# Seven products instead of eight for eight k tiles of an FFN down projection

## The chip, the cores and the metric

The kernel runs on one core of a Trainium2 chip. The metric is the device time of one execution in microseconds (us). TensorE (PE, with its weight loads PEld), VectorE (DVE), ScalarE (ACT), GpSimd (POOL) and SyncE (SP, here only a DMA queue) each work through their own instructions in program order and wait for one another at semaphores.

## The reference, cut to what matters

A decoder block of one layer, 512 tokens, model width 1024, FFN width 2816, all in fp32. The part around the change is the end of it:

```python
f_g, f_u = jnp.split(h2 @ w_ffn_in, 2, axis=-1)
x = x + gate2 * ((jax.nn.silu(f_g) * f_u) @ w_ffn_out)     # (512 x 2816) @ (2816 x 1024)
return rms_norm(x, final_norm_g)
```

`gate2` comes from `silu(c) @ w_ada + b_ada`, the last sixth of its columns.

## The kernel before, in words

The whole kernel is one stream of matmuls. To keep fp32 precision with the faster fp32r matmul, each operand is split into a high part (ACT copies the value to fp32r) and a low part (DVE subtracts the high part from the value), and each product is three matmuls: high by high, high by low, low by high (`mm3`, lines 51 to 55). So each operand block costs ACT one copy and DVE one subtraction before PE can use it. The order of the instructions on every engine is written out by hand; the framework adds the semaphores.

Weights come through a list `stream`. `issue` (line 72) starts the DMA of a chunk into one of three `raw` buffers, `prep` (line 95) makes its high part (line 110) and low part (line 114) in one of three `hi` and `lo` buffers, `ensure` (line 117) does both up to a given chunk, and `get` (line 142) prepares two chunks ahead of the one in use.

The first FFN projection is done, for its later columns, in a loop over q from -1 to 17 (line 1416). An iteration is one 256-column block of `w_ffn_in`, multiplied with the 512 tokens by the Winograd form of Strassen's algorithm: both operands are cut into 2 x 2 blocks, eight added or subtracted blocks are formed, and seven products (`sprod`, line 1410, 12 matmuls of 256 columns each) take the place of eight. The results gather in four PSUM banks, 0 to 3 in odd iterations and 4 to 7 in even ones; some are copied by ACT from one bank to the next (lines 1450 and 1461), others evacuated and added by DVE (lines 1468 to 1476). The operands of iteration q + 1 are made while PE works on q (`s_prep`, line 1275, four steps placed between the products). Even iterations give silu of the gate, odd ones the product `gq` of gate and up part: 22 tiles of 128 rows, 512 tokens wide. Tiles 12 to 15, 16 to 19 and 20, 21 lie together in the buffers E5, E6 and F1.

`last_mod` (line 1320) adds up the last section of `w_ada` in iterations 1 to 8, in buffer E6. `last_gate` (line 1329) splits it, and `sec_tasks` (line 364) sums it over the partitions with two matmuls in one bank (the number in `mbank`) and lets DVE add the bank to `gate_b[2]`; it is done twice, for two halves of 512 columns.

The second FFN projection is lines 1504 to 1554. For each half h of the 1024 output columns it goes through eleven chunks of `w_ffn_out`, two k tiles (256 rows) of 512 columns each. In a chunk each of the four token tiles `tk` gets 2 x 3 matmuls of 512 columns into its own bank (`opt_a_mm`, line 689): 24 matmuls. The first half uses banks 4 to 7. In it `g_split` (line 1355) makes high and low parts of the `gq` tiles just ahead of their use, in buffers that `GHOME` names, and `last_gate` and `sec_tasks` stand behind chunks 3, 5, 6 and 8. At its end `resid` (line 1100) multiplies each bank by the gate, adds it to the residual and lets ACT sum the squares. The second half uses banks 0 to 3, and its last token tile is done as two halves of 256 columns in banks 3 and 7. Its last three chunks are taken token tile by token tile, so that the residual, the final norm and the store of one tile (`finish`, line 1498) go on while PE works on the next.

The first weight chunks of the second projection are issued in iterations 16 and 17 (lines 1425 to 1427), and `s_prep(18)` prepares two of them and four `gq` tiles between the products of iteration 17.

Of the kernel before, what the change touches and what calls it, by code (L numbers as in the profile page):

```python
# [16 lines left out]
S = 512  # L17
D = 1024
# [10 lines left out]
def block_kernel(ctx: ExitStack, tc: tile.TileContext, x, positions, w_ada, b_ada, w_in,  # L29
# [267 lines left out]
    def t512(name, dt=F32):  # L297
        return base.tile([128, 512], dt, name=name, tag="t512", bufs=3)
# [898 lines left out]
    P.dma_start(gate_b[2], rows_bcast(b_ada[0, 5 * D:6 * D], D))  # L1197


    gq = {}  # L1200

    def gtile(m):
        if m not in gq:
            if m < 12:
                gq[m] = base.tile([128, S], F32, name="gq", tag=f"S1_{m + 8 if m < 8 else m - 8}", bufs=1)
            else:
                n = 4 if m < 20 else 2
                t = ffn[0].tile([128, n, S], F32, name="gq", tag=("E5", "E6", "F1")[(m - 12) // 4], bufs=1)
                for e in range(n):
                    gq[m + e] = t[:, e]  # L1210
        return gq[m]

    fs = {}
# [61 lines left out]
    def s_prep(q):  # L1275

        if q >= NQ:
            return [(lambda: ensure(wseq[w_out_at]), lambda: None), (lambda: None, lambda: g_split(1)),
                    (lambda: None, lambda: g_split(3)), (lambda: ensure(wseq[w_out_at + 1]), lambda: g_split(4))]
        ra, rb = sraw[q]  # L1280
        d = sw[q] = {}
        A11, A21, A12, A22 = ra[:, :, 0], ra[:, :, 1], rb[:, :, 0], rb[:, :, 1]

        def a0():
            d["A"] = tuple(base.tile([128, 4, 128], F32R, name="sa", tag=f"S1_{4 + 2 * (q % 2) + e}", bufs=1)
                           for e in range(2))
            A.activation(d["A"][0], A11, AF.Copy)

        def d0():
            V.tensor_add(A21, A21, A22)  # L1290
            V.tensor_sub(d["A"][1], A11, f(d["A"][0]))
            V.tensor_sub(A11, A21, A11)

        def a1():
            d["B"] = s_pair(q, 0)
            A.activation(d["B"][0], rb, AF.Copy)

        def d1():
            V.tensor_sub(d["B"][1], rb, f(d["B"][0]))
            V.tensor_sub(rb, rb, A11[:, :, None, :].to_broadcast([128, 4, 2, 128]))  # L1300

        def a2():
            d["C"] = s_pair(q, 1)
            A.activation(d["C"][0], ra, AF.Copy)

        def d2():
            V.tensor_sub(d["C"][1], ra, f(d["C"][0]))
# [30 lines left out]
    GHOME = [("S1_4", "S1_5"), ("S1_6", "S1_7"), "S2_0", "S2_1", "E2", None, "E4", None, "E1", None, "S2_4", "S2_5",  # L1338
             "E3", None, "S2_6", "S2_7", "S2_2", "S2_3", "E7", None, "E0", None]
    spare = []  # L1340

    def g_home(m):
        h = GHOME[m]
        if h is None:
            return spare.pop()
        if isinstance(h, tuple):
            return [base.tile([128, S], F32R, name="gs", tag=t, bufs=1) for t in h]
        if h[0] == "S":
            t = base.tile([128, 2, S], F32R, name="gs", tag=h, bufs=1)
        else:  # L1350
            t = ffn[0].tile([128, 4, S], F32R, name="gs", tag=h, bufs=1)
            spare.append((t[:, 2], t[:, 3]))
        return t[:, 0], t[:, 1]

    def g_split(upto):
        while len(gT) < min(upto, 22):
            m = len(gT)
            hi, lo = g_home(m)
            split(hi, lo, gq[m])
            gT[m] = (hi, lo)  # L1360


    pf = [[bank(b, "pf") for b in bs] for bs in ((0, 1), (2, 3))]
# [52 lines left out]
    for q in range(-1, NQ):  # L1416
        g, u = 2 + q // 2, q % 2
        d = sw[q]
        s_issue(q + 2)
        pre = s_prep(q + 1)  # L1420
        half_of = lambda t, e: tuple(v[:, :, e] for v in t)
        S2_, S1_, A12, A22, S4_, S3_ = (half_of(d[k], e) for k in "CBD" for e in range(2))
        R = [bank(k + 4 * (q % 2 == 0), "R")[:, :256] for k in range(4)]
        ps = [ffn[0].tile([128, 256], F32, name="ps", tag="rt", bufs=2) for _ in range(2)]
        if q >= NQ - 2:
            st["limit"] = W_FO[0][2] if q == NQ - 2 else 1 << 30
            ensure(st["prep"] - 1)
        t0, t1 = slice(0, 256), slice(256, 512)
        if u:
            dst = [gtile(2 * g + m) for m in range(2)]  # L1430
        else:
            fs[0], fs[1] = t512("fs"), t512("fs")
            dst = fs
        cur = dict(fs)

        def out_direct(m, p, u=u, dst=dict(enumerate([dst[0], dst[1]])), cur=cur):
            if u:
                V.tensor_mul(dst[m][:, t0], cur[m][:, t0], p)
# [11 lines left out]
        A.activation(R[1], R[0], AF.Copy)  # L1450
# [22 lines left out]
        V.tensor_add(dst[1][:, t1], R[3], ps[1])  # L1473
        sprod(R[1], S4_, HB[1, 1], False)
        out_late(1)
        V.tensor_add(dst[0][:, t1], R[1], ps[0])
# [5 lines left out]
    while left:  # L1482
        left.pop(0)()


    fng = ffn[0].tile([128, D], F32, name="fng", tag="F0", bufs=1)
    P.dma_start(fng, rows_bcast(final_norm_g, D))
    xo = []

    def scale_g(c0, n, tk):  # L1490
# [7 lines left out]
    def finish(tk):  # L1498
        A.activation(xo[tk][:, 640:], xo[tk][:, 640:], AF.Copy, scale=r2[:, tk:tk + 1])
        V.tensor_scalar(xo[tk][:, :640], xo[tk][:, :640], r2[:, tk:tk + 1], None, op0=OP.mult)  # L1500
        for c, q in ((slice(0, 640), SY), (slice(640, 1024), A)):
            q.dma_start(out[tk * 128:(tk + 1) * 128, c], xo[tk][:, c])

    for h in range(2):
        pb = [bank(4 - 4 * h + tk, "pfo") for tk in range(4)]
        pb.append(bank(7, "pfo") if h else None)
        ids = W_FO[h]
        for n_, i in enumerate(ids[:-3] if h else ids):
            kts = stream[i]["kts"]
            if h == 0:  # L1510
                g_split(kts[-1] + 1)
            hi, lo = get(i)
            if h == 0:
                g_split(kts[-1] + 4)
            for tk in range(4):
                if h and tk == 3:
                    for z in range(2):
                        c = slice(256 * z, 256 * z + 256)
                        opt_a_mm(pb[3 + z][:, :256], tk, hi[:, :, c], lo[:, :, c], kts, gT, 22)
                else:  # L1520
                    opt_a_mm(pb[tk], tk, hi, lo, kts, gT, 22)
# [11 lines left out]
        for tk in range(4):  # L1533
            for z in range(2) if tk == 3 else (None,):
                c = slice(0, 512) if z is None else slice(256 * z, 256 * z + 256)
                o = pb[tk] if z is None else pb[3 + z][:, :256]
                for i, (hi, lo) in zip(ids[-3:], ch):
                    opt_a_mm(o, tk, hi[:, :, c], lo[:, :, c], stream[i]["kts"], gT, 22)
# [65 lines left out]
```

## Time and profile before

| what | value |
|---|---|
| median of the 3 runs | 846.37 us (845.7 to 847.01) |
| the profiled execution's own time | 845.96 us |
| its span, first to last instruction | 844.2 us |
| mean granted TensorE clock | 0.998 |
| loop over q ends, second projection begins | 713.44 us from the span's start |
| first half of it ends, second begins | 775.41 us |
| last matmul starts | 836.86 us |

The profile was taken on one execution. Its rows in order of time read: start, duration (both us), engine, line of the kernel, operation, output<-inputs, shape, count, and in brackets the time that the engine was idle before and what ended that idle time. A row of a table by stage reads: stage, its length, the busy time of PE, PEld, DVE, ACT and POOL with the number of instructions, the granted TensorE clock, the share of DMA time and GB/s. The durations of matmuls overlap: the step from one start to the next says what a matmul costs, not its duration.

### The profile page before, as it was taken

To read this page: it belongs to the slowest core of one execution; us is meant where nothing else is said; L and a number is where in the kernel's file an instruction comes from. 1 tells how busy PE (TensorE), PEld (TensorE's weight loads), DVE (VectorE), ACT (ScalarE), POOL (GpSimd) and SP (SyncE) were. 2 spreads that over 40 slices of the span, in tenths; PEclk is the share of its full clock that TensorE was granted. 3 is DMA by queue.
4 is the path that set the end of the run, shared out by engine and by line. 5 is a ranking of instruction groups with operands and counts; after the bars stand their busy time and mean duration, and the time that the engine had idled before them with its cause. 6 is when DMAs were issued, how large, how long until landed. Compare 5 with 4: busy or idle time off the path is not lost.

```text
span 844.2 us, 12940 instructions
## 1 busy us (share of the span) xinstructions
PE 831.0 (98%) x5052; PEld 740.5 (88%) x5052; DVE 638.6 (76%) x1127; ACT 386.4 (46%) x680; POOL 118.6 (14%) x105
## 2 busy tenths in 40 slices
PE   7999999999999999999999999999999999999996
PEld 6888889988888888988888899999999999888885
DVE  7978799798899548886767579899998887446225
ACT  5664445322332236666333455655555555433222
POOL 2060022452354411002210000000000000000001
PEclk9999999999999999999999999999999999999999
DMA  9962362432346641146544033445433333332312
GB/s 299 307 188 78 89 200 78 125 99 81 117 142 187 197 150 51 26 127 233 178 138 149 1 125 100 150 154 163 159 102 115 111 117 107 101 100 75 103 47 99
DMA packets 95644, 109.09 MB, mean 129 GB/s; under 512 B 5584, under 2 KB 76240, under 8 KB 95584
## 3 DMA queue, kind: packets, MB, share of 16 engines
q1 hardware_dynamic: 92480, 101.37, 39.5%
q0 software_dynamic: 2384, 6.10, 2.0%
q8 instruction: 39, 0.64, 0.3%
q10 hardware_dynamic: 720, 0.82, 0.3%
q14 instruction: 21, 0.17, 0.1%
HBM read 105.90 MB, written 2.10 MB: 128 GB/s over the span
## 4 chain that ended last, share of the span: by engine, by line
PE 96%; DMA 1%; DVE 1%; issue 0%; SPq 0%; ACT 0%; POOLq 0%; POOL 0%; DVEq 0%
PE pb L53 9%; PE pb L55 9%; PE pb L54 9%; PE R L53 7%; PE R L54 7%; PE R L55 7%; PE pfo L55 5%; PE pfo L54 5%; PE pfo L53 5%; PE pav L54 2%; PE pav L53 2%; PE pav L55 2%; PE po L54 2%; PE pgb L53 2%; PE pgb L54 2%; PE pgb L55 2%
## 5 line engine op out<-in xcount | busy, mean ns | idle before, releaser
L110 ACT ACTIVATE hi<-raw 128x1024 fp32r<-128x1024 f32 (+2 forms) x93 | 96.1, 1037 | 135.7 <-PE pfo L55 67.7
L114 DVE TENSOR_TENSOR lo<-raw,hi 128x1024 fp32r<-128x1024 f32 (+2 forms) x53 | 65.4, 1239 | 75.0 <-ACT hi L110 74.9
L114 POOL TENSOR_TENSOR lo<-raw,hi 128x1024 fp32r<-128x1024 f32 x33 | 83.4, 2531 | 212.9 <-ACT hi L110 207.2
L53 PE MATMUL pb<-h,hi 128*128 128x512 f32 x192 | 76.4, 398 | 0.0
L54 PE MATMUL pb<-hl,hi 128*128 128x512 f32 x192 | 75.8, 395 | 0.0
L55 PE MATMUL pb<-h,lo 128*128 128x512 f32 x192 | 75.8, 395 | 0.0
L55 PE MATMUL pfo<-hi,gs 128*128 128x512 f32 (+1 forms) x198 | 73.0, 369 | 0.0
L53 PE MATMUL pfo<-hi,gs 128*128 128x512 f32 (+1 forms) x198 | 73.0, 369 | 0.0
L54 PE MATMUL pfo<-lo,gs 128*128 128x512 f32 (+1 forms) x198 | 73.0, 369 | 0.0
L53 PE MATMUL R<-tb,sx 128*128 128x256 f32 x160 | 45.2, 282 | 0.0
L54 PE MATMUL R<-tb,sx 128*128 128x256 f32 x160 | 45.1, 282 | 0.0
L55 PE MATMUL R<-tb,sx 128*128 128x256 f32 x160 | 45.0, 281 | 0.0
L55 PEld LDWEIGHTS pb<-h,lo 128*128 128x128 f32 x192 | 36.0, 188 | 8.7
L54 PEld LDWEIGHTS pb<-hl,hi 128*128 128x128 f32 x192 | 36.1, 188 | 8.3
L53 PEld LDWEIGHTS pb<-h,hi 128*128 128x128 f32 x192 | 36.0, 188 | 8.3
L55 PEld LDWEIGHTS pfo<-hi,gs 128*128 128x128 f32 x198 | 37.2, 188 | 6.8
L53 PEld LDWEIGHTS pfo<-hi,gs 128*128 128x128 f32 x198 | 37.3, 188 | 6.7
L54 PEld LDWEIGHTS pfo<-lo,gs 128*128 128x128 f32 x198 | 37.2, 188 | 6.7
L55 PE MATMUL R<-tb,lo 128*128 128x256 f32 x144 | 40.3, 280 | 0.0
L53 PE MATMUL R<-tb,hi 128*128 128x256 f32 x144 | 40.3, 280 | 0.0
L54 PE MATMUL R<-tb,hi 128*128 128x256 f32 x144 | 40.2, 279 | 0.0
L175 DVE SCALAR_TENSOR_TENSOR acc<-mraw,cols,acc 128x512 f32<-128x512 f32 x38 | 31.7, 835 | 9.3 <-DMA mraw<-in_w_ada_dram 8.5
(345 smaller groups left out, 2536.3 us busy)
## 6 DMA issues: line engine op xcount, KB each, us to landing
raw<-in_w_ffn_in_dram SPq DMA_DIRECT2D x44, 512.0 KB, 4.2
raw<-in_w_in_dram SPq DMA_DIRECT2D x40, 512.0 KB, 3.8
mraw<-in_w_ada_dram SPq DMA_DIRECT2D x22, 512.0 KB, 4.0
raw<-in_w_ffn_out_dram SPq DMA_DIRECT2D x22, 512.0 KB, 3.8
s<-in_w_ada_dram SPq DMA_DIRECT2D x30, 256.0 KB, 5.5
raw<-in_w_ada_dram SPq DMA_DIRECT2D x10, 512.0 KB, 4.5
raw<-in_w_proj_a_dram SPq DMA_DIRECT2D x8, 512.0 KB, 4.9
raw<-in_w_proj_b_dram SPq DMA_DIRECT2D x8, 512.0 KB, 3.5
```

The source lines that it names most:

```text
L53: T.matmul(o, wh, rh, start=start, stop=False, **kw)
L54: T.matmul(o, wh, rlo, start=False, stop=False, **kw)
L55: T.matmul(o, wlo, rh, start=False, stop=stop, **kw)
L110: A.activation(hi[:, :m], e["raw"][:, :m], AF.Copy)
L114: e["lo"].tensor_sub(lo[:, :m], e["raw"][:, :m], f(hi[:, :m]))
L175: V.scalar_tensor_tensor(o, w, cs[:, j:j + 1], o, op0=OP.mult, op1=OP.add)
```

## The change

Eight of the 22 k tiles (12 to 19) leave the stream of chunks. They are treated as a product of a 512 x 1024 matrix (tokens by those rows) and a 1024 x 1024 one, each cut into 2 x 2 blocks: A11, A12, A21, A22 of 256 tokens by 4 tiles, and B11 to B22 of 4 tiles by 512 columns. With S1 = A21 + A22, S2 = S1 - A11, S3 = A22 - S2 (in A11's place), S4 = A12 - S2 (in A21's place), T1 = B12 - B11, T2 = B22 - T1, T3 = B22 - B12, T4 = B21 - T2 (all by DVE, in place), seven products (`zprod`, 24 matmuls of 512 columns each) go into all eight banks: A11 B11, S1 T1, S2 T2, A12 B21, S3 T3, S4 B22, A22 T4. Three ACT copies and evacuations and two DVE additions join them (`z_copy`, `z_out`, `z_add`). Each of the four weight blocks is loaded as two pieces of two k tiles in buffers of its own. What was `s_prep(18)` is now `z_first`, which prepares B11, A11, S1 and T1 during iteration 17. The other 14 k tiles (seven chunks a half) are accumulated on top, with no first matmul that clears a bank. `last_gate` and `sec_tasks` move behind iterations 9 and 10, with both halves in bank 3. The first half uses banks 4, 7, 1, 2, the second 5, 6, 0, 3; since bank 7 holds no sum for the second half, ACT copies the upper 256 columns of bank 3 into it first. The first chunk of `w_ffn_out` is issued after the sixth product.

```diff
-    W_FO = [[add_w(w_ffn_out, [k, k + 1], 512 * h, 512) for k in range(0, 22, 2)] for h in range(2)]
+    KZ, KC = (list(range(12, 16)), list(range(16, 20))), list(range(12)) + [20, 21]
+    W_FO = [[add_w(w_ffn_out, KC[k:k + 2], 512 * h, 512) for k in range(0, len(KC), 2)] for h in range(2)]
...
         if q >= NQ:
-            return [(lambda: ensure(wseq[w_out_at]), lambda: None), (lambda: None, lambda: g_split(1)),
-                    (lambda: None, lambda: g_split(3)), (lambda: ensure(wseq[w_out_at + 1]), lambda: g_split(4))]
+            return z_first()
...
-    def last_gate(half):
-        ah, al = t512("ah", F32R), t512("al", F32R)
-        split(ah, al, acc[5, half])
-        acc[5, half] = al
-        sec_done.append((5, half, 0, ah))
+    def last_gate():
+        t = ffn[0].tile([128, 4, S], F32R, name="ahl", tag="E6", bufs=1)
+        for half in range(2):
+            ah, al = t[:, 2 * half], t[:, 2 * half + 1]
+            split(ah, al, acc[5, half])
+            acc[5, half] = al
+            sec_done.append((5, half, 0, ah))
...
+    ZW = {"T1": ("E2", "E4"), "T2": ("E1", "E3"), "T3": ("E0", "E7"), "T4": ("E2", "E4")}
+    ZA = {"A11": 0, "S1": 4, "S2": 6, "A12": 0, "S3": 4, "S4": 6, "A22": 0}
...
+    def w_hi(key, c, src):
...
+        for t, hi in z_parts(zr[src, c], zw[key, c][0]):
+            A.activation(hi, t, AF.Copy)
+
+    def w_lo(key, c, src):
+        for t, hi, lo in z_parts(zr[src, c], *zw[key, c]):
+            V.tensor_sub(lo, t, f(hi))
...
+    def a_hi(key):
+        za[key] = tuple(base.tile([128, 4, 256], F32R, name="za", tag=f"S2_{ZA[key] + e}", bufs=1) for e in range(2))
+        A.activation(za[key][0], a_block(AT_[key]), AF.Copy)
+
+    def a_lo(key):
+        V.tensor_sub(za[key][1], a_block(AT_[key]), f(za[key][0]))
...
+    def z_first():
+        return [(lambda: w_hi("B11", 0, "B11"), lambda: w_lo("B11", 0, "B11")),
+                (lambda: (a_hi("A11"), w_hi("B11", 1, "B11")), lambda: (a_lo("A11"), w_lo("B11", 1, "B11"))),
+                (lambda: None, lambda: (a_sum("S1"), w_sub("B11", "B12", "B11", 0))),
+                (lambda: (w_hi("T1", 0, "B11"), a_hi("S1")),
+                 lambda: (w_lo("T1", 0, "B11"), a_lo("S1"), w_sub("B11", "B12", "B11", 1)))]
...
         if q >= NQ - 2:
-            st["limit"] = W_FO[0][2] if q == NQ - 2 else 1 << 30
-            ensure(st["prep"] - 1)
+            z_issue(("B11", "B12")[q - NQ + 2])
...
+        if q == NQ - 1:
+            z_issue("B21")
...
+        if q == 9:
+            last_gate()
+        if q == 10:
+            mbank[0] = 3
+            sec_tasks(True)
+    z_issue("B22")
...
+    Z, ZB = {}, ((4, 7), (5, 6), (1, 2), (0, 3))
+
+    def zprod(k, ka, kw, start):
+        if start:
+            Z[k] = [bank(ZB[k][e], "pfo") for e in range(2)]
+        (ah, al) = za[ka]
+        for c in range(2):
+            wh, wl = zw[kw, c]
+            for e in range(2):
+                o = slice(e * 128, (e + 1) * 128)
+                for j in range(2):
+                    mm3(Z[k][e], (ah[:, 2 * c + j, o], al[:, 2 * c + j, o]), (wh[:, j], wl[:, j]),
+                        start and c + j == 0, c + j == 2, skip_group_check=True)
...
+    zprod(0, "A11", "B11", True)
+    w_hi("T1", 1, "B11")
+    w_lo("T1", 1, "B11")
+    while left:
+        left.pop(0)()
+    a_sum("S2")
+    z_copy(1, 0)
+    w_sub("B11", "B22", "B11", 0)
+    zprod(3, "S1", "T1", True)
+    a_hi("S2")
+    a_lo("S2")
+    w_hi("T2", 0, "B11")
+    w_lo("T2", 0, "B11")
+    w_sub("B11", "B22", "B11", 1)
+    w_hi("T2", 1, "B11")
+    w_lo("T2", 1, "B11")
+    z_out(3)
+    zprod(1, "S2", "T2", False)
+    a_hi("A12")
+    a_lo("A12")
+    for c in range(2):
+        w_hi("B21", c, "B21")
+        w_lo("B21", c, "B21")
+    for c in range(2):
+        w_sub("B12", "B22", "B12", c)
+    a_sum("S4")
+    w_hi("T3", 0, "B12")
+    z_copy(2, 1)
+    zprod(0, "A12", "B21", False)
+    w_lo("T3", 0, "B12")
+    a_sum("S3")
+    a_hi("S3")
+    a_lo("S3")
+    w_hi("T3", 1, "B12")
+    w_lo("T3", 1, "B12")
+    z_add(1, 3)
+    zprod(2, "S3", "T3", False)
+    a_hi("S4")
+    a_lo("S4")
+    for c in range(2):
+        w_hi("B22", c, "B22")
+        w_lo("B22", c, "B22")
+    for c in range(2):
+        w_sub("B11", "B21", "B11", c)
+    z_out(2)
+    zprod(1, "S4", "B22", False)
+    a_hi("A22")
+    a_lo("A22")
+    w_hi("T4", 0, "B11")
+    w_lo("T4", 0, "B11")
+    w_hi("T4", 1, "B11")
+    w_lo("T4", 1, "B11")
...
+    st["limit"] = 1 << 30
+    ensure(W_FO[0][0])
+    zprod(2, "A22", "T4", False)
+    g_split(2)
+    z_add(3, 2)
...
-        pb = [bank(4 - 4 * h + tk, "pfo") for tk in range(4)]
-        pb.append(bank(7, "pfo") if h else None)
+        pb = [Z[h][0], Z[h][1], Z[2 + h][0], Z[2 + h][1]]
         ids = W_FO[h]
+        if h:
+            pb.append(bank(7, "pfo"))
+            A.activation(pb[4][:, :256], pb[3][:, 256:], AF.Copy)
...
-            if h == 0 and n_ in (3, 6):
-                last_gate(n_ // 6)
-            if h == 0 and n_ in (5, 8):
-                mbank[0] = n_ // 8
-                sec_tasks(True)
```

More of the change, by code (lines that the diff above doesn't have):

```diff
@@ L1210, in gtile @@
                     gq[m + e] = t[:, e]
+                gz.append(t)
         return gq[m]
@@ L1355, in g_split, with z_issue @@
     def g_split(upto):
-        while len(gT) < min(upto, 22):
-            m = len(gT)
-            hi, lo = g_home(m)
+        while len(gT) < min(upto, len(KC)):
+            m = KC[len(gT)]
+            hi, lo = g_home(len(gT))
             split(hi, lo, gq[m])
             gT[m] = (hi, lo)
+    zr, zw, za = {}, {}, {}
+    ZW = {"T1": ("E2", "E4"), "T2": ("E1", "E3"), "T3": ("E0", "E7"), "T4": ("E2", "E4")}
+    ZA = {"A11": 0, "S1": 4, "S2": 6, "A12": 0, "S3": 4, "S4": 6, "A22": 0}
+    def z_issue(name):
+        kh, h = {"B11": (0, 0), "B12": (0, 1), "B21": (1, 0), "B22": (1, 1)}[name]
+        for c in range(2):
+            if name == "B11" or name == "B12" and c == 0:
+                t = base.tile([128, 2, S], F32, name="raw", tag="raw", bufs=RAWB)
+                ts = [t]
+            elif name == "B12":
+                ts = [ffn[0].tile([128, 2, S], F32, name="zraw", tag="F0", bufs=1)]
+            elif name == "B22":
+                ts = [base.tile([128, 2, S], F32, name="zraw", tag=f"S2_{2 + c}", bufs=1)]
+            else:
+                ts = [base.tile([128, 1, S], F32, name="zraw", tag=f"S1_{4 + 2 * c + e}", bufs=1) for e in range(2)]
+            k = KZ[kh][2 * c]
+            for t in ts:
+                n = t.shape[1]
+                SY.dma_start(t, w_ffn_out[k * 128:(k + n) * 128, h * 512:h * 512 + 512].rearrange("(j p) n -> p j n", p=128))
+                k += n
+            zr[name, c] = ts
@@ new lines, in z_parts @@
+    def z_parts(ts, *others):
+        o = 0
+        for t in ts:
+            n = t.shape[1]
+            yield (t,) + tuple(x_[:, o:o + n] for x_ in others)
+            o += n
+    def w_hi(key, c, src):
+        if key in ZW:
+            t = ffn[0].tile([128, 2, 2, S], F32R, name="zw", tag=ZW[key][c], bufs=1)
+            zw[key, c] = (t[:, 0], t[:, 1])
+        else:
+            zw[key, c] = tuple(base.tile([128, 2, S], F32R, name=n, tag=n, bufs=3) for n in ("hi", "lo"))
+        for t, hi in z_parts(zr[src, c], zw[key, c][0]):
+            A.activation(hi, t, AF.Copy)
@@ new lines, in w_lo, with w_sub, a_block @@
+    def w_lo(key, c, src):
+        for t, hi, lo in z_parts(zr[src, c], *zw[key, c]):
+            V.tensor_sub(lo, t, f(hi))
+    def w_sub(o, a, b, c):
+        (o_,), (b_,) = zr[o, c], zr[b, c]
+        for a_, ob, bb in z_parts(zr[a, c], o_, b_):
+            V.tensor_sub(ob, a_, bb)
+    def a_block(name):
+        kh, th = {"A11": (0, 0), "A21": (0, 1), "A12": (1, 0), "A22": (1, 1)}[name]
+        return gz[kh][:, :, th * 256:(th + 1) * 256]
+    AT_ = {"A11": "A11", "A12": "A12", "A22": "A22", "S1": "A21", "S4": "A21", "S2": "A11", "S3": "A11"}
@@ new lines, in a_hi, with a_sum @@
+    def a_hi(key):
[3 more added lines that the diff above has]
+        V.tensor_sub(za[key][1], a_block(AT_[key]), f(za[key][0]))
+    def a_sum(key):
+        a = {n: a_block(AT_[n]) for n in AT_}
+        if key == "S1":
+            V.tensor_add(a["S1"], a_block("A21"), a["A22"])
+        elif key == "S2":
+            V.tensor_sub(a["S2"], a["S1"], a["A11"])
+        elif key == "S4":
+            V.tensor_sub(a["S4"], a["A12"], a["S2"])
+        else:
+            V.tensor_sub(a["S3"], a["A22"], a["S2"])
@@ L1481, in block_kernel @@
             last_mod(q - 1)
[L1482 to L1487, printed above, removed]
+        if q == 9:
[4 more added lines that the diff above has]
+    z_issue("B22")
     xo = []
@@ new lines, in z_copy, with z_out, z_add @@
+    def z_copy(dst, src):
+        Z[dst] = [bank(ZB[dst][e], "pfo") for e in range(2)]
+        for e in range(2):
+            A.activation(Z[dst][e], Z[src][e], AF.Copy)
+    def z_out(src):
+        Z["s", src] = [t512("ps") for _ in range(2)]
+        for e in range(2):
+            A.activation(Z["s", src][e], Z[src][e], AF.Copy)
+    def z_add(dst, src):
+        for e in range(2):
+            V.tensor_add(Z[dst][e], Z[dst][e], Z["s", src][e])
+    zprod(0, "A11", "B11", True)
+    w_hi("T1", 1, "B11")
@@ new lines, in block_kernel @@
+    for c in range(2):
[17 more added lines that the diff above has]
+        w_lo("B22", c, "B22")
+    for c in range(2):
+        w_sub("B11", "B21", "B11", c)
@@ L1504, in block_kernel @@
+    z_out(2)
[6 more added lines that the diff above has]
+    w_lo("T4", 1, "B11")
+    fng = ffn[0].tile([128, D], F32, name="fng", tag="F0", bufs=1)
+    P.dma_start(fng, rows_bcast(final_norm_g, D))
+    st["limit"] = 1 << 30
[3 more added lines that the diff above has]
+    z_add(3, 2)
     for h in range(2):
-        pb = [bank(4 - 4 * h + tk, "pfo") for tk in range(4)]
@@ L1537, in block_kernel @@
                 for i, (hi, lo) in zip(ids[-3:], ch):
-                    opt_a_mm(o, tk, hi[:, :, c], lo[:, :, c], stream[i]["kts"], gT, 22)
+                    opt_a_mm(o, tk, hi[:, :, c], lo[:, :, c], stream[i]["kts"], gT, 22, False)
                 n = c.stop - c.start
```

19 lines of the change are left out of this document (9 added, 10 removed).

## The prediction

> **What bounds the kernel now.** I read the page first: TensorE is busy for 98% of the span and makes 96% of the chain that ended last.
>
> ```profile
> span 844.2 us, 12940 instructions
> PE 831.0 (98%) x5052; PEld 740.5 (88%) x5052; DVE 638.6 (76%) x1127; ACT 386.4 (46%) x680; POOL 118.6 (14%) x105
> PE 96%; DMA 1%; DVE 1%; issue 0%; SPq 0%; ACT 0%; POOLq 0%; POOL 0%; DVEq 0%
> ```
>
> Then the table by stage, cut at the marks of the code: one iteration of the loop over q (633.74 to 643.70 is q = 10, 693.50 to 703.46 is q = 16), the last one (q = 17), and the first chunk of the second FFN projection.
>
> ```profile
> 633.74:643.70 9.96, 9.96 (x86) 9.96 (x85) 8.90 (x14) 4.75 (x8) 0.00 (x0) 1.00 0.34 106
> 693.50:703.46 9.96, 9.96 (x86) 9.96 (x85) 8.90 (x14) 4.75 (x8) 0.00 (x0) 1.00 0.36 102
> 703.46:713.44 9.98, 9.98 (x87) 9.98 (x85) 5.11 (x8) 7.25 (x14) 0.55 (x1) 1.00 0.47 150
> 713.30:775.80 62.50, 62.50 (x273) 50.81 (x272) 32.85 (x47) 22.07 (x34) 0.00 (x0) 1.00 0.33 101
> ```
>
> The columns are PE, PEld, DVE, ACT, POOL busy. PE never waits; DVE has little room in the loop (8.90 of 9.96) and much in the projection (32.85 of 62.50). So only PE work can be saved, and each us that PE is made to wait costs a us.
>
> **The saving.** Two rows twelve matmuls apart give the pitch of a 128x512 matmul:
>
> ```profile
> 829.67 0.40 PE L55 MATMUL pfo<-hi,gs 128*128 128x512 f32 x1
> ...
> 832.47 0.40 PE L55 MATMUL pfo<-hi,gs 128*128 128x512 f32 x1
> ```
>
> 2.80 / 12 = 0.2333 us. Eight k tiles cost 8 x 8 output tiles x 3 = 192 matmuls; seven products cost 7 x (4 k tiles x 2 token tiles x 3) = 168. The change removes 24: **-5.6 us**. Each product takes 24 x 0.2333 = 5.6 us of PE. Everything else is whether DVE, ACT and the DMAs deliver the operands on time.
>
> **What is added for DVE and ACT.** Their prices:
>
> ```profile
> 688.02 1.23 DVE L1299 TENSOR_TENSOR lo<-raw,hi 128x1024 fp32r<-128x1024 f32 x1 [1.45 <-ACT hi L1296]
> 689.28 1.23 DVE L1300 TENSOR_TENSOR raw<-raw 128x1024 f32<-128x1024 f32 x1
> 690.42 1.22 DVE L1307 TENSOR_TENSOR lo<-raw,hi 128x1024 fp32r<-128x1024 f32 x1
> 693.37 0.41 DVE L1438 TENSOR_TENSOR gq<-fs,R 128x256 f32<-128x256 f32 x1
> 693.70 0.42 DVE L1473 TENSOR_TENSOR gq<-R,ps 128x256 f32<-128x256 f32 x1
> 695.28 0.68 DVE L1290 TENSOR_TENSOR raw<-raw 128x512 f32<-128x512 f32 x1
> 695.88 0.69 DVE L1291 TENSOR_TENSOR sa<-raw,sa 128x512 fp32r<-128x512 f32 x1
> 704.42 1.04 ACT L110 ACTIVATE hi<-raw 128x1024 fp32r<-128x1024 f32 x1
> 705.37 0.37 ACT L1450 ACTIVATE R<-R 128x256 f32<-128x256 f32 x1
> 705.49 1.23 DVE L114 TENSOR_TENSOR lo<-raw,hi 128x1024 fp32r<-128x1024 f32 x1 [1.43 <-ACT hi L110]
> ```
>
> DVE on 1024 elements: 1.22 us, the next starts 1.14 after it; on 512: 0.60; on 256: 0.34. ACT on 1024: 1.05, next after 0.96. A consumer starts 0.03 after its producer (705.46 to 705.49). The operand blocks (4 x 256 tokens, or 2 x 512 weights) are all 1024 elements.
>
> I lay the queues out in program order from q = 17 (703.46), with ACT free at 704.42 and the first copy where L110 stands now. Without waits PE would end q = 17 at 713.44 and begin products two to seven at 719.04, 724.64, 730.24, 735.84, 741.44, 747.04.
>
> DVE's queue: low part of B11 (first half) 705.50 to 706.64; it waits for A11's high copy, which ACT does after the evacuation of product two (706.78 to 707.83); four large operations from 707.86 to 712.42; a wait for T1's high copy, which itself needs the fourth, to 713.61; three large to 717.03; five small ones of the loop to 718.95; T1's second low part, a small one, S2 and B22-T1 to 722.71; lows of S2 and T2 and a subtraction to 726.18; a wait for ACT; **T2's second low part at 727.37 to 728.59**. Then A12's low part at 729.39 (a wait again), four halves of B21 (2.4 us) to 732.93, three large (two B22-B12, S4) to 736.35, T3's low part and S3 (done 738.71), the wait for S3's high copy (738.74 to 739.79), and **S3's low part at 739.82 to 741.04**. In all 22 large x 1.14 = 25.1, four halves 2.4, six small 2.3 and waits for ACT of 5.7 us, from 705.50: 741.0.
>
> PE against it. A11·B11 and S1·T1 do not wait (T1's second low part, 720.2, is wanted at 722.1). S2·T2 waits for T2: 0.28 + 0.67 = 0.95. A12·B21 waits for B21's low part: 0.43. S3·T3 could begin at 737.21; its first matmul waits for S3's high copy until 739.82, its third for the low part until 741.07: 2.61 + 0.78 = 3.39. S4·B22 and A22·T4 then find their operands (745.7 and 751.5, wanted at 746.2 and 751.8). **+4.8 us**. Bounds: if all waits for ACT vanished (5.7) nothing of it is left, 0; if each large operation were followed after 1.26 us instead of 1.14, as 688.02 to 689.28 is, 22 x 0.12 = 2.6 more, 7.4. I take 4.8, since 1.14 is the commoner step.
>
> **The weight stream begins anew.** Now the first chunks of w_ffn_out lie ready early (SP issues them from 691.66 on); in the change the first chunk's raw buffer is T4's, free at 751.48 once its low part is made.
>
> ```profile
> 691.66 75.00 SPq L92 DMA_DIRECT2D raw<-in_w_ffn_out_dram  x15
> raw<-in_w_ffn_out_dram SPq DMA_DIRECT2D x22, 512.0 KB, 3.8
> s<-in_w_ada_dram SPq DMA_DIRECT2D x30, 256.0 KB, 5.5
> ```
>
> 751.48 + 3.8 to 4.2 lands at 755.4; copy 1.05, low part 1.22 (757.8), low part of the first g tile (758.4). PE ends its last product at 757.40, and does two matmuls meanwhile: **+0.6**, between 0 (a wait that the late products before it take up) and 2 (a landing after 5.5 us, the slower row). The second chunk needs its g tiles at 763.6 and 764.3; they end at 763.1 and 763.7, queued behind both lows: nothing, if all goes so.
>
> **The gate at q = 10.** last_gate and its four matmuls leave the projection, where each pair (0.47 us, no wait behind it) had its own bank and stage, and go behind q = 9 and q = 10. Both pairs use bank 3: the second waits for DVE's add of the first.
>
> ```profile
> 643.58 0.28 PE L55 MATMUL R<-tb,lo 128*128 128x256 f32 x1
> 643.70 0.28 PE L53 MATMUL R<-h,sa 128*128 128x256 f32 x1
> 643.89 0.41 DVE L1476 TENSOR_TENSOR fs<-R,ps 128x256 f32<-128x256 f32 x1
> 644.22 0.68 DVE L1290 TENSOR_TENSOR raw<-raw 128x512 f32<-128x512 f32 x1
> 747.46 0.69 DVE L377 TENSOR_TENSOR gate2b<-gate2b,mod 128x512 f32<-128x512 f32 x1 [2.39 <-PE mod L375]
> ```
>
> Pair one runs 643.70 to 644.17. The two splits (1.3 us of DVE) leave DVE some 0.3 late at that place, the rest is taken by its idle time; so the add runs 644.5 to 645.2: **+1.05**, between 0.8 (DVE not late) and 2 (late by all of the 1.3). The add also holds DVE's next step until pair two is added, 0.3 more than PE's own delay, within DVE's spare 1.06 us an iteration.
>
> **The second half (h = 1).** Its fourth token tile is split over banks 3 and 7, and bank 7's part must first be copied by ACT out of bank 3. In ACT's queue that copy stands behind the four squares of the first half's residual.
>
> ```profile
> 775.41 0.39 PE L53 MATMUL pfo<-hi,gs 128*128 128x512 f32 x1
> ...
> 779.53 0.28 PE L53 MATMUL pfo<-hi,gs 128*128 128x256 f32 x1
> 780.24 0.28 PE L53 MATMUL pfo<-hi,gs 128*128 128x256 f32 x1
> 780.19 0.63 ACT L1105 ACTIVATE rt<-xr 128x512 f32<-128x512 f32 x1 [1.67 <-DVE xr L1104]
> 780.82 1.99 ACT L110 ACTIVATE hi<-raw 128x1024 fp32r<-128x1024 f32 x2
> ```
>
> h = 1 begins at 775.41; PE wants bank 3 4.12 us later (779.53) and bank 7 at 780.24. The copy can run at 780.82, where L110 stands now, to 781.2. If matmuls into bank 3 wait for a reader of that bank's other half, PE waits 1.7 us; if not, 1.0. **+1.7**: the kernel gives the two halves banks of their own, so the trace shows no case of a shared one. The Trainium skill, PSUM — Partial Sum Buffer, section on bank collisions, says to guard by bank and not by address; by that rule it is 1.7, without it 1.0; no row here shows it.
>
> **Sum.** -5.6 + 4.8 + 0.6 + 1.05 + 1.7 = **+2.6 us**. The profiled execution took 845.96 us, of which 1.8 lie around the span; 845.96 + 2.6 = **848.6**. The median of the runs shown, 846.37, is 0.4 above that execution.
>
> **Rivals.**
> 1. *DVE keeps up, and the kernel is faster.* Place: DVE's queue from q = 17 to S3. Price: its waits for ACT, 5.7 us in my layout, would not arise, the products would not wait, and the sum is -5.6 + 0.6 + 1.05 + 1.7 = -2.3: 843.7. It decides from 2.6 us less of such waits. For it: ACT is busy 4.75 of 9.96 us and could copy early. Against it: five of these copies need the subtraction just before them in DVE's own queue, or follow an evacuation.
> 2. *The waits at the banks do not come* (gate and copy cost nothing): -5.6 + 4.8 + 0.6 = -0.2: 845.8, no change. Against: both orders are written in the queues.
> 3. *The clock falls in the long wait* before S3·T3 (2.6 us, then 0.8). The trace has a fall after the last matmul:
>
> ```profile
> 836.86 0.28 PE L55 MATMUL pfo<-hi,gs 128*128 128x256 f32 x1
> 838.00:840.00 2.00, 0.00 (x0) 0.00 (x0) 1.32 (x5) 0.95 (x3) 0.66 (x1) 1.00 0.39 143
> 840.00:842.00 2.00, 0.00 (x0) 0.00 (x0) 0.11 (x1) 0.17 (x1) 0.00 (x0) 0.76 0.51 199
> 842.00:844.00 2.00, 0.00 (x0) 0.00 (x0) 0.00 (x0) 0.00 (x0) 0.00 (x0) 0.50 0.17 63
> ```
>
> Full until 840, mean 0.76 in the next 2 us, then 0.50: half speed from about 841.0, 3.9 us after PE's end (837.1). Two waits of 3.4 us in all are just short of that. If it falls for as long as it took to fall here, 3.9 us at half speed add 2.0: 850.6. The Trainium skill, TensorE: Matmul & The Clock Gate, Part 1, has the gate close after an idle window of about 3.4 us that runs freely; the trace's 3.9 agrees. By that rule 2.6 us is too short unless the wait grows by a third.
>
> **How the numbers follow.** Forecast +2.6 with its own bounds (846.5 to 851): 0.62. Rival 1 0.13, rival 2 0.15, rival 3 0.10. A measurement of this kernel tells about 0.2% (1.7 us) from no change. Faster is rival 1, 0.13; within 0.2% is rival 2 and 0.10 of the forecast's low end, 0.25; slower 0.62. The range begins between rivals 1 and 2, at 844.5, and ends at 852.0, above rival 3 and above the forecast with DVE's upper bound (848.6 + 2.6 = 851.2).
>
> **What would show it.** In the changed profile: PE rows of the seven products 0.233 apart, 168 of them; a PE wait of about 1 us for DVE before q = 11; one of 2 to 3 us before S3·T3 with DVE busy almost without pause and waiting only for ACT; the last w_ffn_out issues beginning after T4's low part; PE waiting for ACT in the first chunk of h = 1. The prediction is wrong if DVE is idle for long before S3, or if PE's wait there is under 1 us or the clock there is below 1.0.

## The result, and the profile after

The change made the kernel slower: 849.46 us (median of 6 runs, 849.1 to 850.88) against 846.71 us (6 runs of the kernel before, 845.7 to 847.1), a ratio of 1.0036 with a 95% interval of 1.0023 to 1.0049. The span of the profiled execution grew from 844.2 to 847.4 us, by 3.2; forecast were 2.6.

The page of the changed kernel answers the first lines of the page before:

```profile
span 847.4 us, 12890 instructions
PE 829.5 (98%) x5004; PEld 735.9 (87%) x5004; DVE 664.4 (78%) x1152; ACT 399.5 (47%) x696; POOL 118.4 (14%) x105
PE 89%; DVE 5%; DMA 2%; issue 1%; ACT 1%; SPq 1%; POOLq 0%; POOL 0%; DVEq 0%; ACTq 0%
```

PE has 48 matmul instructions fewer (24 full matmuls, and 24 more because 24 of the old ones stood as pairs of halves), but its share of the last chain fell from 96% to 89%: DVE, DMA and ACT are on it now. Where PE waits is read from its rows in order of time. A step from one start to the next above the pitch (0.233 us for 128x512, 0.119 for 128x256) is time lost; the bracket names who ended it. First the gate behind q = 10 (mod is its bank):

```profile
643.89 0.39 PE L377 MATMUL mod<-ahl,onesr 128*128 128x512 f32 x1
645.10 0.50 PE L376 MATMUL mod<-ahl,onesr 128*128 128x512 f32 x1 [0.82 <-DVE gate2b L379]
645.43 0.40 PE L377 MATMUL mod<-ahl,onesr 128*128 128x512 f32 x1
```

645.10 - 643.89 - 0.23 = 0.98 us for DVE's add of the first half, and 0.10 for the first matmul after the wait (0.33 instead of 0.23 to the next). Then the products S2 T2 and S3 T3 (zw is a weight operand, za a token operand):

```profile
729.92 0.39 PE L53 MATMUL pfo<-zw,za 128*128 128x512 f32 x1
730.74 0.50 PE L54 MATMUL pfo<-zw,za 128*128 128x512 f32 x1 [0.43 <-DVE zw L1408]
...
738.78 0.40 PE L55 MATMUL pfo<-hi,za 128*128 128x512 f32 x1
741.88 0.51 PE L53 MATMUL pfo<-zw,za 128*128 128x512 f32 x1 [2.71 <-ACT za L1425]
742.23 0.40 PE L54 MATMUL pfo<-zw,za 128*128 128x512 f32 x1
743.14 0.80 PE L55 MATMUL pfo<-zw,za 128*128 128x512 f32 x1 [0.52 <-DVE za L1428]
743.74 0.63 PE L53 MATMUL pfo<-zw,za 128*128 128x512 f32 x1
744.16 0.63 PE L54 MATMUL pfo<-zw,za 128*128 128x512 f32 x1
...
746.65 0.40 PE L54 MATMUL pfo<-zw,za 128*128 128x512 f32 x1
746.89 0.39 PE L55 MATMUL pfo<-zw,za 128*128 128x512 f32 x1
```

S2 T2 loses 1.1 us in two places (the second is shown). S3 T3 waits for S3's high copy and then for its low part: 2.87 + 0.12 + 0.68 = 3.7. And from 743.14 on the matmuls take 0.43 from start to start instead of 0.23, until 746.65: 1.6 us more. DVE's rows of that time show what it did meanwhile:

```profile
727.11 1.22 DVE L1414 TENSOR_TENSOR raw<-zraw,raw 128x1024 f32<-128x1024 f32 x1
729.46 1.23 DVE L1408 TENSOR_TENSOR zw<-raw,zw 128x1024 fp32r<-128x1024 f32 x1 [1.13 <-ACT zw L1404]
731.37 1.23 DVE L1428 TENSOR_TENSOR za<-gq,za 128x1024 fp32r<-128x1024 f32 x1 [0.69 <-ACT za L1425]
...
739.47 1.22 DVE L1439 TENSOR_TENSOR gq<-gq 128x1024 f32<-128x1024 f32 x1
741.87 1.23 DVE L1428 TENSOR_TENSOR za<-gq,za 128x1024 fp32r<-128x1024 f32 x1 [1.18 <-ACT za L1425]
```

It has no idle time but the turns to ACT, 1.13, 0.69 and 1.18 us in these rows (line 1439 forms S3, line 1428 its low part). ACT has more room: from 725 to 738 us it is busy for 7.82 us and DVE for 11.18, although ACT's copies and evacuations of banks are four steps of two banks each, not three. The last wait is that for the copy in the first chunk of the second half; these rows are of ACT and PE:

```profile
804.29 0.63 ACT L1107 ACTIVATE rt<-xr 128x512 f32<-128x512 f32 x1 [1.39 <-DVE xr L1106]
804.92 0.36 ACT L1686 ACTIVATE pfo<-pfo 128x256 f32<-128x256 f32 x1
803.61 0.40 PE L55 MATMUL pfo<-hi,gs 128*128 128x512 f32 x1
805.34 0.39 PE L53 MATMUL pfo<-hi,gs 128*128 128x256 f32 x1 [1.33 <-ACT pfo L1686]
```

The copy (line 1686) runs right behind the fourth square, and the matmul that waits for it is the first into bank 3, not the first into bank 7: 1.5 + 0.1 us.

| term, us | forecast | profile after |
|---|---|---|
| 24 matmuls fewer | -5.6 | -5.8 |
| gate behind q = 10 | 1.05 | 1.1 |
| q = 17 | 0 | 0.1 |
| S2 T2 | 0.95 | 1.1 |
| A12 B21 | 0.43 | 0 |
| S3 T3, waiting | 3.4 | 3.7 |
| S3 T3, slow matmuls | 0 (rival 3: 2.0) | 1.6 |
| weight stream begins anew | 0.6 | 0 |
| copy into bank 7 | 1.7 | 1.6 |
| sum | 2.6 | 3.4 (span: 3.2) |

The -5.8 is what remains between PE's rows: from the end of q = 17 to the last matmul 123.42 us before (713.44 to 836.86), of them 0.93 for the gate, and 124.69 after (715.54 to 840.23), of them 8.0 of the losses above.

### The profile page after: what moved, and what is told of

It reads as the page before. It is cut to its first block, busy times and chain, and to the rows that moved or that the text cites. A ratio compares the mean times of both kernels' runs of the same rounds, so it can differ in the third digit from the quotient of the medians.

```text
span 847.4 us, 12890 instructions
## 1 busy us (share of the span) xinstructions
PE 829.5 (98%) x5004; PEld 735.9 (87%) x5004; DVE 664.4 (78%) x1152; ACT 399.5 (47%) x696; POOL 118.4 (14%) x105
## 4 chain that ended last, share of the span: by engine, by line
PE 89%; DVE 5%; DMA 2%; issue 1%; ACT 1%; SPq 1%; POOLq 0%; POOL 0%; DVEq 0%; ACTq 0%
PE pb L53 9%; PE pb L55 9%; PE pb L54 9%; PE R L53 7%; PE R L54 7%; PE R L55 7%; PE pfo L55 3%; PE pfo L53 3%; PE pfo L54 3%; PE pav L54 2%; PE pav L55 2%; PE pav L53 2%; PE pgb L53 2%; PE po L54 2%; PE pgb L54 2%; PE pgb L55 2%
## 5 line engine op out<-in xcount | busy, mean ns | idle before, releaser
L110 ACT ACTIVATE hi<-raw 128x1024 fp32r<-128x1024 f32 (+2 forms) x85 | 87.8, 1035 | 106.9 <-PE pfo L55 34.7
L114 DVE TENSOR_TENSOR lo<-raw,hi 128x1024 fp32r<-128x1024 f32 (+2 forms) x45 | 55.7, 1242 | 51.7 <-ACT hi L110 51.5
L53 PE MATMUL pfo<-hi,gs 128*128 128x512 f32 (+1 forms) x126 | 46.5, 369 | 1.3 <-ACT pfo L1686 1.3
L55 PE MATMUL pfo<-hi,gs 128*128 128x512 f32 (+1 forms) x126 | 46.4, 368 | 0.0
L54 PE MATMUL pfo<-lo,gs 128*128 128x512 f32 (+1 forms) x126 | 46.4, 368 | 0.0
L54 PE MATMUL pav<-lo,h 128*128 128x256 f32 x128 | 35.8, 279 | 0.0
L55 PE MATMUL pav<-hi,hl 128*128 128x256 f32 x128 | 35.8, 279 | 0.0
L53 PE MATMUL pav<-hi,h 128*128 128x256 f32 x128 | 35.8, 279 | 0.0
```

What stands on the lines that cost most here:

```text
L53: T.matmul(o, wh, rh, start=start, stop=False, **kw)
L54: T.matmul(o, wh, rlo, start=False, stop=False, **kw)
L55: T.matmul(o, wlo, rh, start=False, stop=stop, **kw)
L110: A.activation(hi[:, :m], e["raw"][:, :m], AF.Copy)
L114: e["lo"].tensor_sub(lo[:, :m], e["raw"][:, :m], f(hi[:, :m]))
```

## The experiments

Times are medians; "above" and "below" are against the kernel before, measured alongside on the same chip (846.56 us for the first four, 846.25 for the next four, 846.34 for the last). My theory was the sum above: five waits and a fall of the clock, each with a cause of its own.

**The gate's halves apart.**

```diff
-        if q == 9:
-            last_gate()
-        if q == 10:
+        if q in (9, 11):
+            last_gate(q // 11)
+        if q in (10, 12):
             mbank[0] = 3
             sec_tasks(True)
```

> The gate's two halves are split behind q = 9 and q = 11 and multiplied behind q = 10 and q = 12, each alone in bank 3; nothing else differs from the changed kernel, which was 2.75 us slower than the one before by the medians. Theory: the wait of the second pair for DVE's add (PE idle from 644.12 to 645.10, then 0.1 for the first matmul behind it) is gone and nothing takes its place, so 1.1 us less: 1.65 to 1.9 above the kernel before, and no PE step over 0.3 us between two matmuls before q = 17. Rival: PE waits there because DVE is late from the splits, whichever bank is used: the wait is split in two and the time stays at 2.75 above.

848.47 us (846.96 to 849.54, 11 runs), 1.9 above, ratio 1.0023 (1.0014 to 1.0031). The trace has no step with over 0.3 us lost ahead of q = 17. The second pair's wait for the add of the first, in the bank that they shared, was the cause; two banks for the two pairs were not tried. What I had not expected is the spread of 2.6 us; in the profiled execution PE waits as long before S3 T3 as in the changed kernel and the clock does not fall:

```profile
737.79 0.40 PE L55 MATMUL pfo<-hi,za 128*128 128x512 f32 x1
740.90 0.51 PE L53 MATMUL pfo<-zw,za 128*128 128x512 f32 x1 [2.71 <-ACT za L1427]
...
742.16 0.50 PE L55 MATMUL pfo<-zw,za 128*128 128x512 f32 x1 [0.52 <-DVE za L1430]
742.50 0.39 PE L53 MATMUL pfo<-zw,za 128*128 128x512 f32 x1
```

**The copy early.**

```diff
                 resid(pb[tk], 0, 512, 0, tk, gate_b[2])
+                if tk == 1:
+                    b7.append(bank(7, "pfo"))
+                    A.activation(b7[0][:, :256], Z[3][1][:, 256:], AF.Copy)
                 scale_g(0, 512, tk)
...
         if h:
-            pb.append(bank(7, "pfo"))
-            A.activation(pb[4][:, :256], pb[3][:, 256:], AF.Copy)
+            pb.append(b7[0])
```

> ACT's copy of half of bank 3 into bank 7 is written behind the residual of the second token tile of the first half (the last reader of bank 7), ahead of the squares of tiles two and three, not behind all four. Theory: PE's wait of 1.6 us in the first chunk of the second half comes from the place of the copy in ACT's queue alone and goes: 1.1 to 1.4 above the kernel before. Rival: the wait is for bank 3 or 7 to come free from DVE, and moving the copy does not help: 2.75 above.

847.99 us (11 runs), 1.4 above, ratio 1.0022 (1.0013 to 1.0031). PE does not wait there any more (the step into the first matmul of bank 3 is 804.80 to 805.03, the pitch): the place in ACT's queue was the cause.

**Sums on GpSimd.**

```diff
-            V.tensor_sub(a["S4"], a["A12"], a["S2"])
+            P.tensor_sub(a["S4"], a["A12"], a["S2"])
...
-            V.tensor_sub(a["S3"], a["A22"], a["S2"])
+            P.tensor_sub(a["S3"], a["A22"], a["S2"])
...
-        w_sub("B12", "B22", "B12", c)
+        w_sub("B12", "B22", "B12", c, P)
```

> Four of DVE's subtractions (the two halves of T3, S4 and S3) are done by GpSimd, idle in this stage, in the same places of the program. Theory: the product S3 T3 waits because DVE's queue is 4.56 us (4 x 1.14) too long; without them S3's low part is there before PE asks. Both PE's wait there (3.7 us) and the slow matmuls behind it (1.5 us) go: 2.75 - 5.2 = 2.4 us faster than the kernel before, with the wait at S2 T2 (1.1 us) left. Rival: GpSimd at 2.5 us an operation hands S3 over too late or slows DVE while both work, and PE waits as long: about 2.75 above.

851.54 us (5 runs), 5.0 above, ratio 1.0062 (1.0048 to 1.0076): the theory's number is missed by over 7 us. The rival's mechanism holds, but its price was too low as well. Rows of GpSimd and of DVE:

```profile
718.22 2.96 POOL L1414 TENSOR_TENSOR raw<-zraw,raw 128x1024 f32<-128x1024 f32 x1 [223.68 <-DVE za L1428]
719.16 0.41 DVE L1559 TENSOR_TENSOR gq<-R,ps 128x256 f32<-128x256 f32 x1
719.61 1.85 DVE L1528 TENSOR_TENSOR gq<-gq,fs 128x256 f32<-128x256 f32 x1
...
726.78 3.19 POOL L1437 TENSOR_TENSOR gq<-gq 128x1024 f32<-128x1024 f32 x1 [3.05 <-PE pfo L55]
731.20 3.22 POOL L1439 TENSOR_TENSOR gq<-gq 128x1024 f32<-128x1024 f32 x1 [1.23 <-DVE za L1428]
727.73 3.32 DVE L1428 TENSOR_TENSOR za<-gq,za 128x1024 fp32r<-128x1024 f32 x1
730.97 1.21 DVE L1408 TENSOR_TENSOR zw<-raw,zw 128x1024 fp32r<-128x1024 f32 x1
732.11 3.38 DVE L1414 TENSOR_TENSOR raw<-zraw,raw 128x1024 f32<-128x1024 f32 x1
```

A DVE operation that starts while GpSimd works ends about 1.1 us after GpSimd does (731.05 after 729.97, 735.49 after 734.42): it stands still until then and then takes its time. In the same way two of the loop's small operations took 1.85 and 2.18 instead of 0.42. Operations with one operand in PSUM (R is a bank) were not held up: the one at 719.16 took 0.41 us in the midst of GpSimd's 718.22 to 721.18. DVE lost 2.10 + 2.16 + 1.43 + 1.76 = 7.5 us and saved 4.56. So this run does not show that DVE's queue was not the bound; it made the queue longer, and PE waited 5.6 us in S2 T2 alone; S3 T3 then had no wait, but it began at 746.17 instead of 741.88. The Trainium skill, SBUF — State Buffer, section Who interferes with whom, says that a DVE instruction with two SBUF inputs contends with a GpSimd instruction that reads SBUF, that one with at most one such input does not, and that the ports they share are an exclusive lock; the rows agree.

**Zeros in the wait.**

```diff
+    for _ in range(10):
+        T.matmul(Z[0][0], zr0, za["A12"][0][:, 0:2].rearrange("p a n -> p (a n)"), start=False, stop=False, skip_group_check=True)
     zprod(2, "S3", "T3", False)
```

> Ten matmuls with a stationary tile of zeros (they add nothing) stand in bank 4 ahead of the product S3 T3 and fill 2.3 us of its wait; one small DVE instruction at the start makes the zeros. Theory: the matmuls behind the wait take 0.43 instead of 0.23 us because the clock fell in the wait; with PE busy the clock stays, the granted clock of this stage reads 1.00, and 1.5 us are saved: 1.2 above the kernel before. Rival: these matmuls are slow since DVE and ACT read and write the same memory at that time: their step stays 0.43 and the time 2.75 above.

847.66 us (847.54 to 848.05, 11 runs), 1.1 above, ratio 1.0014 (1.0005 to 1.0023). The steps behind the wait are 0.23 again while DVE and ACT do what they did, so the slow matmuls were the clock's and not the memory's; and the spread of the runs is 0.5 us. The table by stage of the changed kernel (two rows), of this one and of the early copy (three rows); the column before the last two is the granted clock:

```profile
741.00:744.00 3.00, 1.60 (x4) 1.06 (x5) 2.13 (x2) 3.00 (x4) 0.00 (x0) 0.86 0.45 161
744.00:747.00 3.00, 3.00 (x9) 2.36 (x9) 3.00 (x5) 1.62 (x2) 0.55 (x1) 0.57 0.38 131
```

```profile
741.00:744.00 3.00, 2.08 (x8) 1.12 (x7) 2.24 (x2) 3.00 (x4) 0.00 (x0) 1.00 0.41 153
```

```profile
741.00:744.00 3.00, 1.51 (x3) 0.80 (x4) 1.82 (x3) 2.66 (x3) 0.00 (x0) 0.61 0.55 175
744.00:747.00 3.00, 3.00 (x8) 2.35 (x8) 3.00 (x4) 2.19 (x3) 0.55 (x1) 0.50 0.19 66
747.00:750.00 3.00, 3.00 (x12) 2.38 (x11) 3.00 (x5) 0.10 (x1) 0.00 (x0) 0.75 0.30 109
```

Read as time at half speed (the share of the clock lost, times the length of the stage, over 0.5): (0.14 + 0.43) x 3 / 0.5 = 3.4 us in the changed kernel, none with the zeros, (0.39 + 0.50 + 0.25) x 3 / 0.5 = 6.8 in the early copy's execution. With a wait of the same length before S3 T3 the clock stayed up in the execution with the gate apart, fell for 3.4 us in the changed kernel's and for twice that in the early copy's.

**Two more lows.**

```diff
     a_hi("A12")
-    a_lo("A12")
+    for _ in range(3):
+        a_lo("A12")
```

> The changed kernel with the low part of A12 made three times over instead of once: two more DVE operations of 1024 elements (1.14 us each) in its queue before S3, same results. Theory: from S2 T2 to S3 T3 PE follows DVE's queue, so the time grows by the 2.3 us in full (some of it may move to a wait at A12 B21, which now has none), and the clock falls as before or for longer: 5.0 to 6 above the kernel before, against 2.75 for the change. Rival: PE waits for ACT's copies, which are not longer: no more than 0.3 above the change.

851.18 us (5 runs), 4.9 above, ratio 1.0060 (1.0046 to 1.0074): 2.2 above the change for 2.3 us of DVE. PE now waits 2.15 us at A12 B21 and 1.62 + 0.69 at S3 T3. In the profiled execution, counted from the start of q = 17, the third matmul of S3 T3 starts 2.5 us later than in the change (745.58 instead of 743.14, while q = 17 itself starts 0.1 earlier). So PE follows DVE's queue here, and ACT's copies only as far as they follow DVE. The clock fell again, after a wait of no more than 1.98 us, but ahead of the wait for S3, which took up its price: this execution is only 1.0 us longer by its span (848.4), and it is the fastest of the five. Rows of PE, and the table by stage:

```profile
733.31 0.40 PE L53 MATMUL pfo<-hi,za 128*128 128x512 f32 x1
735.69 0.50 PE L54 MATMUL pfo<-lo,za 128*128 128x512 f32 x1 [1.98 <-DVE lo L1408]
```

```profile
725.00:738.00 13.00, 10.47 (x41) 7.55 (x40) 11.11 (x12) 5.90 (x9) 0.00 (x0) 0.96 0.00 0
738.00:741.00 3.00, 3.00 (x9) 2.33 (x9) 3.00 (x4) 2.03 (x3) 0.00 (x0) 0.60 0.02 5
```

**The new order.**

```diff
     w_sub("B11", "B22", "B11", 1)
+    a_sum("S4")
     w_hi("T2", 1, "B11")
     w_lo("T2", 1, "B11")
     z_out(3)
     zprod(1, "S2", "T2", False)
+    a_sum("S3")
     a_hi("A12")
     a_lo("A12")
     for c in range(2):
         w_hi("B21", c, "B21")
         w_lo("B21", c, "B21")
-    for c in range(2):
-        w_sub("B12", "B22", "B12", c)
-    a_sum("S4")
+    a_hi("S3")
+    w_sub("B12", "B22", "B12", 0)
     w_hi("T3", 0, "B12")
     z_copy(2, 1)
+    a_lo("S3")
     zprod(0, "A12", "B21", False)
     w_lo("T3", 0, "B12")
-    a_sum("S3")
-    a_hi("S3")
-    a_lo("S3")
+    w_sub("B12", "B22", "B12", 1)
     w_hi("T3", 1, "B12")
     w_lo("T3", 1, "B12")
```

> The same operations in another order, nothing added: S4 is formed while DVE waits for the high copy of T2's second half, S3 before A12's parts, S3's low part while ACT copies T3's first half, and T3's second half only after that. Theory: DVE then reaches S3's and T3's first low parts at about the time PE asks for them (lows some 3.5 us earlier), PE's wait at S3 T3 falls from 3.7 to under 0.7 us and the clock no longer falls (1.5 us); DVE stays late, so up to 1.2 us come back at S4 B22 and A22 T4. 2.75 - 3.0 - 1.5 + 1.2 = 0.5 faster than the kernel before, between 1.5 faster and 0.5 slower. Rival: DVE's work as a whole is too long for the seven products, whatever its order: the wait of 3.7 us moves to S4 B22 and A22 T4, and only the clock's 1.5 us are saved: 1.2 above.

845.62 us (11 runs), 0.6 below, ratio 0.9993 (0.9985 to 1.0002): as fast as the kernel before within what can be told, 3.4 us better than the change. DVE works without a break where it had turns to ACT (the table by stage: 13.00 of 13.00 busy, 11.18 in the changed kernel):

```profile
725.00:738.00 13.00, 12.46 (x53) 9.30 (x52) 13.00 (x14) 8.41 (x13) 0.00 (x0) 1.00 0.00 1
738.00:741.00 3.00, 3.00 (x15) 2.41 (x14) 1.87 (x3) 1.54 (x3) 0.00 (x0) 1.00 0.33 113
```

PE's wait before S3 T3 is gone and the clock stays at 1.00. What comes back is 0.3 and 0.1 within S3 T3, 0.7 at S4 B22 and 0.3 at A22 T4; the waits in S2 T2, 1.1, stay.

**The new order, the gate apart and the early copy together.** The diff is the sum of three above.

> The new order together with the gate's two halves apart (first run) and the early copy (second run). Theory: the terms add, since each is a wait of PE of its own: the time of the new order alone less 1.1 less 1.6, so about 3.2 us faster than the kernel before. Rival: waits that are taken away come back, as DVE's queue only shifts: less than 1 us faster than the new order alone.

842.79 us (842.61 to 843.22, 5 runs), 3.5 below, ratio 0.9960 (0.9947 to 0.9972). The terms add. This version beats both kernels.

**The gate apart, the early copy and the zeros, old order.**

> The changed kernel's own order, with the gate apart, the early copy and the ten matmuls with zeros in the wait before S3 T3, so that the waits at S2 T2 and S3 T3 are the only ones left and the clock stays. Theory: -5.6 for the 24 matmuls, + 1.1 + 3.7 + 0.1: 0.7 faster than the kernel before. Rival: some of the slowdown of the change has a cause outside the terms named, and 1 us or more of it is left: 0.5 or more above the kernel before.

845.02 us (11 runs), 1.2 below, ratio 0.9986 (0.9977 to 0.9994), 0.5 better than the sum of the terms: no slowdown is left that the terms don't name.

**No sums.** In `w_sub` and `a_sum` of the kernel with all three edits, a `return` ahead of the subtractions.

> The kernel of the run with the new order, the gate apart and the early copy, with the twelve sums and differences of blocks (S1 to S4, both halves of T1 to T4) left out: the seven products are multiplied from blocks that were not combined, so the output isn't the block's; all high and low parts, copies, loads and matmuls stay. Theory: DVE then has 12 x 1.14 = 13.7 us less to do and no product waits, so the time shows the bare saving of the 24 matmuls: 5.5 to 5.9 us below the kernel before, and no step over 0.3 us beyond the pitch among the products. Rival: a part of the waits is owed to ACT's copies or to the loads, and stays: less than 4.5 us below the kernel before.

840.07 us (5 runs), 6.3 below, ratio 0.9927 (0.9913 to 0.9941); its span is 838.3 us, 5.9 under that of the kernel before. The one step left over 0.1 us beyond the pitch from q = 11 on is that of 0.11 in q = 17. That is the bare saving of seven products, and the sums' price in the best order found is what lies between this and the run of all three: 842.79 - 840.07 = 2.7 us of waits.

## Why the prediction was right, and where not

**The saving** (step one) was right: -5.6 forecast, -5.8 in PE's rows, -5.9 by the span of the run without sums.

**DVE's queue** was the bound that the prediction laid out, and the largest term: 4.8 forecast for all products, 1.1 + 3.7 = 4.8 measured. The low part of S3 came 36.4 us after q = 17 began (741.87 - 705.45), against 739.82 - 703.46 = 36.4 in the layout, and T2's second low part 24.0 after it (729.46 - 705.45) against 23.9 (727.37 - 703.46). Two more DVE operations cost 2.2 of their 2.3 us, and the new order, which only fills the turns to ACT, took the wait away. That the term came out equal is luck in one respect: inside it the 0.43 at A12 B21 was wrong, and waits of 0.15 and 0.3 us more in S2 T2 and S3 T3 stand against it. I let PE wait for both k tiles of B21's low part, but each is an instruction of its own and PE waits only for the one it reads.

**The gate** (1.05 forecast, 1.1 measured) **and the copy** (1.7, 1.6) were right, in place and size; each went from PE's rows when its cause was removed, and the medians fell by 0.8 and 1.3 us. The choice left open between bank and address is settled for this kernel: PE waits ahead of the first matmul into bank 3, whose other half ACT reads.

**The weight stream** was wrong: "in the change the first chunk's raw buffer is T4's". It is B12's, the first of the three whose last reader (T3's first low part, 738.33 to 739.55) comes up; SP, which does nothing but start DMAs, issues the chunk then, although it is written behind the sixth product; ACT copies it without a wait, and PE loses nothing. The sign that I had named for it, issues that begin after T4's low part (752.84 in DVE's rows), did not come. These rows are of SP and ACT:

```profile
739.58 24.65 SPq L92 DMA_DIRECT2D raw<-in_w_ffn_out_dram  x6
753.46 1.05 ACT L110 ACTIVATE hi<-raw 128x1024 fp32r<-128x1024 f32 x1
```

**The clock** was the step that failed most: the sum puts the fall at nothing, and by the sign that I had named myself (the clock before S3 T3 below 1.0; it is 0.86 and then 0.57) the prediction is wrong in this. Rival 3 came about and was given 0.10, because I read one fall, 3.9 us after the last matmul, as the time that a fall needs. Waits of 2.71 and 0.52 us were enough, and in another run 1.98; what counts is how much of one stretch of 3.4 us is idle (last section). Its price (2.0 in the rival; 1.6 in the profile; 1.65 between the medians of the change, 2.75 above, and of the zeros, 1.1 above) was about right. That the forecast came within 0.6 us of the span is in part luck: the clock's 1.6 and 0.5 in other places stand against 0.6 for the stream, 0.4 for A12 B21, 0.2 more saving and 0.2 less behind the last matmul.

**Rival 1** did not come about in the change. The new order shows that its place was right, by another way than it said: the operations stayed, and their order put the sums into the turns to ACT. Its price was not reached: 0.6 below the kernel before instead of 2.3. Rival 2 did not hold: both waits came.

## What to carry to other kernels

Seven products for eight move work from the engine that is the bound to one that must then form, split and hand over the sums in time: lay out that engine's queue in program order against the product starts before writing the code, and put independent sums where it would wait for another engine. A wait that is short against the saving can be made dearer by the clock behind it. And an evacuation or copy that was harmless becomes a wait when its bank is reused at once, or when it stands in the queue behind work that waits for something else.

## What the runs showed of the hardware

- **The clock falls for stretches of 3.4 us, on a grid of its own.** Half speed lasted 3.4 us in the changed kernel, 6.8 in the early copy's execution, and (0.04 x 13 + 0.40 x 3) / 0.5 = 3.4 in the run with two more lows. The falls keep step: in the changed kernel the one ends at 746.56, and the next, after the last matmul, begins at 845.54, 29 times 3.413 us later. Cut at this grid, the table by stage reads, for the changed kernel, two more lows, the early copy, and the gate apart (counted back by 29 and 30 stretches from the fall at its end, 842.24):

```profile
739.73:743.14 3.41, 0.74 (x2) 0.30 (x2) 2.23 (x3) 2.36 (x3) 0.00 (x0) 1.00 0.45 154
743.14:746.56 3.42, 3.42 (x8) 2.77 (x9) 3.42 (x5) 2.48 (x3) 0.55 (x1) 0.50 0.19 62
```

```profile
733.58:736.99 3.41, 1.43 (x7) 1.08 (x7) 3.38 (x6) 0.00 (x0) 0.00 (x0) 1.00 0.00 0
736.99:740.41 3.42, 3.42 (x10) 2.64 (x9) 3.42 (x4) 1.80 (x3) 0.00 (x0) 0.50 0.02 5
```

```profile
738.24:741.65 3.41, 1.49 (x7) 0.87 (x5) 3.01 (x3) 0.84 (x3) 0.00 (x0) 1.00 0.08 12
```

```profile
736.42:739.84 3.42, 1.77 (x8) 1.10 (x6) 3.28 (x3) 0.85 (x3) 0.00 (x0) 1.00 0.01 4
739.84:743.25 3.41, 1.83 (x7) 1.21 (x8) 2.37 (x3) 3.41 (x4) 0.00 (x0) 1.00 0.43 150
```

  Half speed followed a stretch in which PE was idle for 2.67, 1.98 or 1.92 us. With the gate apart the wait is as long, but the grid cuts it into 1.65 and 1.58, and the clock stays at 1.00. So, in these executions, the place of the wait in the grid decided whether it cost some 1.6 us more; where between 1.65 and 1.92 the line lies, and why the early copy's fall lasted two stretches, no run here shows. The 3.9 us that the prediction read from the kernel before were the rest of one stretch and a whole one (837.64 to 841.05). The Trainium skill, TensorE: Matmul & The Clock Gate, Part 1, names a window of about 3.4 us that runs freely; the lengths agree, and so does the chance from run to run. It also wants a whole window idle, which here none of these waits filled: the measurement decides that less is enough.
- **GpSimd holds up DVE** when both subtract with two operands in SBUF: 1.22 us became 3.3. DVE's operations with one operand in PSUM kept their 0.41.
- **The first matmul after a wait** takes 0.10 to 0.12 us more than the pitch (0.33 from 645.10 to 645.43).
